# One more unit of filler work ahead of the first attention head in a two-layer transformer kernel

## The chip, the cores and the metric

The kernel runs on one core of one Trainium2 chip. The metric is the device time of one execution in microseconds (us); of several executions the median is given. The core has five engines that run their own instruction queues in order and wait for each other by semaphores: TensorE (PE in the rows; PEld is its weight load), VectorE (DVE), ScalarE (ACT), GpSimd (POOL) and SyncE (SP), which here only issues DMAs.

## The reference

Two layers act on 256 tokens of width 2048, with a context of 256 more. Layer 0 is a Fourier mixer, layer 1 is attention; each has adaptive scale, shift and gate, and an output projection from 4096 to 2048. The change lies in layer 1: 64 query heads of width 64, 8 key/value heads, a sink in the softmax, and the result multiplied by silu(z).

```python
def _attend_with_sink(q, k, v, sink, mask=None):
    s = jnp.einsum('bqhgd,bkhd->bhgqk', q, k).astype(jnp.float32) * (ATTN_HEAD_DIM ** -0.5)
    ...
    p = jax.nn.softmax(jnp.concatenate([s, sk], axis=-1), axis=-1)[..., :-1]
    return jnp.einsum('bhgqk,bkhd->bqhgd', p.astype(v.dtype), v)

def _attention_branch(h, hc, w_in, sink, rows, cols, need_ctx):
    q, k, v, z = jnp.split(h @ w_in, [D_BRANCH, D_BRANCH + kvw, D_BRANCH + 2 * kvw], axis=-1)
    ...
    y = jnp.moveaxis(o, 0, 1).reshape(b, n, D_BRANCH) * jax.nn.silu(z)
```

After it come `y @ w_out[1]`, the gated residual and a final RMS norm. There are 512 keys per query: 256 tokens and 256 of the context.

## The kernel before

Nearly all arithmetic is float32 made of two parts: a weight tile is split into a high part `wh` (a cast on ACT, L66) and a remainder `wl` (a subtraction on DVE, L67), and three matmuls take the place of one (`mm3`, L145 to L147). Some weights of layer 0 and of the key/value projection are split into two float16 parts instead.

The attention stage of layer 1 interleaves two streams of work.

**The filler.** `units()` lists 140 units of projection work. Eight units make the query projection of one key/value head's group of eight query heads ("q"); two units make one 128-wide block of z ("z", L1386 and L1388). The list is q0, q1, z0 to z3, q2, z4 to z7, and so on to q7 and z24 to z31, and then 12 units ("o") of the output projection, each two of the 32 steps `k` of its first 512 columns. `emit_unit()` emits the next unit and prepares the weights of the one after (DMA on SP, cast on ACT, subtraction on DVE). When the list is empty it emits nothing. A unit of q or o is 12 matmuls, a unit of z is 16 shorter ones.

**The heads.** There are 64 heads `i`. `stage_s(i)` computes the scores: four matmuls (L1422, L1423), the mask and the maximum on DVE (L1424), the exponential on ACT (L1427, L1428), the reciprocal of the sum on DVE (L1429, L1430), and the probabilities `f` as two float16 halves, high by ACT (L1439) and low by DVE (L1440), for two blocks of 128 queries each. For the heads below 62, `f` is then transposed into `ft` by two DMA transposes from SP's queue (L1442), one for each query block. For the last two heads the transposes are matmuls on PE (`stage_t`, L1449) and are copied out of PSUM by ACT and DVE (L1450). `stage_o(i)` multiplies `ft` with the values on PE (8 matmuls, L1457 and L1458), and ACT and DVE add the two halves up (L1463, L1464). After every second head, `emit_y` writes a block of y (L1407), which `y_split` later splits into two parts for the output projection; for the steps `k` below 24 POOL makes the remainder (L67 on POOL), above that DVE.

**The order.** First come `first` units with no head beside them; then 66 steps. Step `i` emits `stage_s(i)`, (for the last two heads) `stage_t(i - 2)`, one unit, `stage_o(i - 2)`, and one unit. So 66 steps have 132 places for units, and with 10 ahead there are 142 places for 140 units: the last two places, both in step 65, stay empty. After the steps the code goes on with `k` = 24 to 31 of the same output projection (four more pieces of that work, which need all of y) and then with the other columns.

That is the order in which the code emits. The build then schedules the emitted instructions, engine by engine, by a timeline of its own; the program holds one fixed order per engine. So a place in the emitted list moves what each engine meets, but not one for one.

In the text, "head 0" is `stage_s(0)` and so on; "scores of head i" are its four matmuls, "output of head i" the eight of L1457 and L1458.

Of the kernel before, what the change touches and what calls it, by code (L numbers as in the profile page):

```python
# [32 lines left out]
def tile_dit(ctx: ExitStack, tc: tile.TileContext, a: dict, out: bass.AP):  # L33
# [1102 lines left out]
    with tc.tile_pool(name="h1", reuse_waits="tile", bufs=16) as h1p:  # L1136
# [94 lines left out]
        with tc.tile_pool(name="at", reuse_waits="tile", bufs=2) as at:  # L1231
# [234 lines left out]
                    obs[blk, 1] = ob  # L1466
                    emit_y(blk)

            first = 10
            for i in range(first):  # L1470
                emit_unit()
                if i == 2:
# [249 lines left out]
```

## Time and profile before

| | us |
|---|---|
| median of 3 runs | 1769.35 (1767.74 to 1769.62) |
| the profiled execution, its own time | 1769.55 |
| span of the profile of that execution | 1767.8 |
| attention stage: first scores, last output of a head (start) | 1127.2, 1608.8 |

The span is the time from the first to the last profiled instruction; the execution's own time has 1.75 us more around it. Rows of the timeline view give the start in us from the span's start, the duration in us (of a merged row with "x4" of all four together), the engine, the line, the operation, `out<-in` with the buffer numbers left out, and in square brackets how long the engine was idle just before and what released it. PE's matmuls overlap: the duration of one is longer than the step from one start to the next, so a pace on PE is read from the starts.

### The profile page before, as it was taken

What the parts mean: (1) busy time and instruction counts of PE and PEld (TensorE: products, weight loads), DVE (VectorE), ACT (ScalarE), POOL (GpSimd) and SP (SyncE); (2) the same over time, 40 slices, a digit from 0 to 9 for tenths busy, and PEclk for the clock granted to TensorE, in tenths of its full rate; (3) what the DMA queues carried; (4) which work ended last, traced back from release to release, by engine and by line L of the source; (5) the groups of instructions that cost most, each with busy time, mean ns of one, the idle gap of its engine ahead of it and who ended that gap; (6) DMA issues with size and microseconds to landing.
All of it is one profiled execution on the core that took longest, in us unless ns stands there. A gap on an engine that the chain in (4) does not pass through costs nothing. (4 is left out here: it accounts for less than half of the span.)

```text
span 1767.8 us, 26608 instructions
## 1 busy us (share of the span) xinstructions
PE 1732.2 (98%) x9517; PEld 1187.7 (67%) x9517; DVE 1406.6 (80%) x2454; ACT 1090.5 (62%) x2069; POOL 331.9 (19%) x440
## 2 busy tenths in 40 slices
PE   6999999999999999999999999999999999999997
PEld 4679999644444444446444746788888888887886
DVE  5779889797677786877797695899999989997455
ACT  5545556477777755465223554687888878895343
POOL 0002111212222214212101001302312230233010
PEclk9999999999999999999999999999999999999999
DMA  9998998778998969977996432588988898887543
GB/s 394 417 356 247 279 278 254 289 286 314 332 305 312 312 228 371 368 267 259 341 316 212 142 137 74 169 215 199 223 207 206 213 215 206 207 212 258 190 167 143
DMA packets 229077, 447.29 MB, mean 253 GB/s; under 512 B 155888, under 2 KB 156288, under 8 KB 202064
## 3 DMA queue, kind: packets, MB, share of 16 engines
q1 hardware_dynamic: 182784, 331.93, 58.3%
q0 software_dynamic: 42016, 106.70, 19.4%
q10 hardware_dynamic: 4144, 6.95, 1.2%
q8 instruction: 75, 1.23, 0.3%
q14 instruction: 58, 0.48, 0.1%
HBM read 400.43 MB, written 12.59 MB: 234 GB/s over the span
## 5 line engine op out<-in xcount | busy, mean ns | idle before, releaser
L67 DVE TENSOR_TENSOR wl<-raw,wh 128x1024 fp32r<-128x1024 f32 x197 | 262.5, 1338 | 108.0 <-ACT wh L66 80.3
L66 ACT CAST wh<-raw 128x1024 fp32r<-128x1024 f32 x197 | 205.5, 1044 | 138.1 <-PE ps L146 97.0
L146 PE MATMUL ps<-act,wf 128*128 128x512 f16 x512 | 194.0, 379 | 0.0
L147 PE MATMUL ps<-act,wf 128*128 128x512 f16 x512 | 191.1, 379 | 0.0
L145 PE MATMUL ps<-act,wf 128*128 128x512 f16 x512 | 189.8, 379 | 0.6 <-ACT wf L137 0.2
L1386 PE MATMUL ps<-h,wh 128*128 128x512 f32 x512 | 185.0, 397 | 0.0
L145 PE MATMUL ps<-y,wf 128*128 128x512 f16 x448 | 169.8, 379 | 0.8 <-ACT wf L137 0.8
L147 PEld LDWEIGHTS <-wf 128*128 128x128 f16 x960 | 93.8, 98 | 114.0 <-DVE wf L138 0.9
L146 PE MATMUL ps<-y,wf 128*128 128x512 f16 x448 | 169.8, 379 | 0.0
L145 PEld LDWEIGHTS <-wf 128*128 128x128 f16 x960 | 93.7, 98 | 113.3 <-ACT wf L137 4.2
L147 PE MATMUL ps<-y,wf 128*128 128x512 f16 x448 | 167.4, 379 | 0.4 <-DVE wf L138 0.4
L146 PEld LDWEIGHTS <-wf 128*128 128x128 f16 x960 | 93.9, 98 | 109.0
L137 ACT ACTIVATE wf<-raw,nrm 128x1024 f16<-128x1024 f32 x56 | 63.4, 1145 | 137.1 <-DVE acc L792 68.5
L1388 PE MATMUL ps<-h,wl 128*128 128x256 f32 x512 | 138.6, 281 | 0.0
L138 DVE SCALAR_TENSOR_TENSOR wf<-raw,tn,wf 128x1024 f16<-128x1024 f32 x64 | 79.8, 1281 | 42.0 <-ACT wf L137 41.9
L1440 DVE SCALAR_TENSOR_TENSOR f<-p,sm,f 128x512 f16<-128x512 f32 x128 | 105.8, 847 | 9.0 <-ACT f L1439 8.7
L790 POOL DMA_DIRECT2D wa<-in_adw x64 | 34.0, 532 | 403.2 <-PE ps L147 149.7
L1427 ACT ACTIVATE p<-ps,mx 128x512 f32<-128x512 f32 x128 | 87.9, 689 | 35.0 <-DVE mx L1424 29.6
L1439 ACT ACTIVATE f<-p,sm 128x512 f16<-128x512 f32 x128 | 88.1, 717 | 34.3 <-DMA ft<-f 15.6
L1386 PEld LDWEIGHTS ps<-h,wh 128*128 128x128 f32 x512 | 96.4, 188 | 19.1
L827 ACT ACTIVATE act<-act 128x512 f32<-128x512 f32 x160 | 98.4, 616 | 6.0 <-DMA act<-in_wo 4.5
L146 PE MATMUL ps<-wl,h 128*128 128x512 f32 x256 | 101.3, 396 | 0.0
(414 smaller groups left out, 4672.8 us busy)
## 6 DMA issues: line engine op xcount, KB each, us to landing
raw<-in_wz SPq DMA_DIRECT2D x64, 1024.0 KB, 5.4
raw<-in_awp SPq DMA_DIRECT2D x32, 1024.0 KB, 12.7
zr<-in_adw SPq DMA_DIRECT2D x64, 512.0 KB, 6.8
wa<-in_adw POOLq DMA_DIRECT2D x64, 512.0 KB, 6.5
act<-in_wo POOLq DMA_DIRECT2D x128, 256.0 KB, 7.5
raw<-in_wo SPq DMA_DIRECT2D x32, 1024.0 KB, 7.7
raw<-in_wq SPq DMA_DIRECT2D x32, 1024.0 KB, 5.2
raw<-in_wu SPq DMA_DIRECT2D x32, 1016.0 KB, 6.5
```

Source lines behind the costliest of these rows:

```text
L66: last_cast[0] = S.copy(h, src).ins
L67: last_sub[0] = eng.tensor_tensor(l, src, h.bitcast(F32), op=ALU.subtract).ins
L138: last_sub[0] = V.scalar_tensor_tensor(w[:, 1], src, up, w[:, 0], op0=ALU.mult, op1=ALU.subtract).ins
L145: PE.matmul(o, wh, xh, start=start, stop=False)
L146: PE.matmul(o, wh, xl, start=False, stop=False)
L147: return PE.matmul(o, wl, xh, start=False, stop=stop).ins
L827: S.activation(t, t, AF.Square, accum_out=c)
L1386: PE.matmul(o[0], wh[:, q], hx1[k], start=k == 0, stop=k == KT - 1)
L1388: PE.matmul(o[0][:, 0:N], wl[:, q], hx1[k][:, 0:N], start=False, stop=False)
L1427: S.activation(pt[tb], so[tb], AF.Exp, bias=mx[:, tb : tb + 1], scale=-1.0, accum_out=sm[:, tb : tb + 1])
L1439: S.activation(f[:, 0:512], pt[tb], AF.Copy, scale=sm[:, tb : tb + 1])
L1440: V.scalar_tensor_tensor(f[:, 512:1024], pt[tb], sm[:, tb : tb + 1], f[:, 0:512], op0=ALU.mult, op1=ALU.subtract)
```

## The change

`first` is 11 instead of 10. So one more unit (the third of q1) stands ahead of head 0, every later unit stands one place earlier among the heads, and three places at the end are empty instead of two: the second place of step 64 and both of step 65. No instruction of the computation is added or removed.

```diff
-            first = 10
+            first = 11
             for i in range(first):
                 emit_unit()
                 if i == 2:
```

**Around head 0, on DVE.** The names are: `sm` the softmax sum, `ps`, `mx` the scores being masked and their maximum (L1424, of the third head here, whose row `ISA mx` reads the maximum out), `wl` the remainder of a weight tile, `f` the probabilities of head 0. Before:

```order
L1429 SCALAR_TENSOR_TENSOR sm_10963<-sm_10963,es_10964 128x2
L1424 ISA ps_11087,mx_11084<-ps_11087,mask_9936,nsink_9940 128x512
L1424 ISA mx_11084 128x1
L1430 RECIPROCAL sm_10963<-sm_10963 128x2
L1424 ISA ps_11091,mx_11084<-ps_11091,mask_9936,nsink_9940 128x512
L67 TENSOR_TENSOR wl_11141<-raw_11138,wh_11140 128x1024
L1440 SCALAR_TENSOR_TENSOR f_10979<-p_10960,sm_10963,f_10979 128x512
L1440 SCALAR_TENSOR_TENSOR f_10983<-p_10961,sm_10963,f_10983 128x512
L67 TENSOR_TENSOR wl_11206<-raw_11138,wh_11205 128x1024
```

The same place now:

```order
L1429 SCALAR_TENSOR_TENSOR sm_10979<-sm_10979,es_10980 128x2
L1430 RECIPROCAL sm_10979<-sm_10979 128x2
L67 TENSOR_TENSOR wl_11128<-raw_11125,wh_11127 128x1024
L1440 SCALAR_TENSOR_TENSOR f_10995<-p_10976,sm_10979,f_10995 128x512
L1424 ISA ps_11103,mx_11100<-ps_11103,mask_9936,nsink_9940 128x512
L1424 ISA mx_11100 128x1
L1440 SCALAR_TENSOR_TENSOR f_10999<-p_10977,sm_10979,f_10999 128x512
L1424 ISA ps_11107,mx_11100<-ps_11107,mask_9936,nsink_9940 128x512
L67 TENSOR_TENSOR wl_11179<-raw_11125,wh_11178 128x1024
```

The masking of the third head's scores moved from ahead of both halves of head 0's `f` to between and behind them. On PE the scores of heads 0 and 1 stand where they stood; those of the third head come after 19 matmuls of filler instead of 7; the output of head 0 keeps its place.

**Around the last head, on DVE.** Here `ps_16520` and `ps_16544` are the output of head 61, `sm`, `f` belong to head 63, `ft_16407` and `ft_16429` are the second query block of head 62's transpose, `ft_16491` and `ft_16513` that of head 63's. Before:

```order
L1464 TENSOR_TENSOR ob_16445<-ps_16520,ot_16529 64x256
L1450 COPY ft_16407<-ps_16568 128x8x128
L1429 SCALAR_TENSOR_TENSOR sm_16476<-sm_16476,es_16477 128x2
L1430 RECIPROCAL sm_16476<-sm_16476 128x2
L1407 SCALAR_TENSOR_TENSOR act_16532<-ob_16445,dsc_9946,th_16019 128x256
L67 TENSOR_TENSOR wl_16579<-raw_16534,wh_16578 128x1024
L1440 SCALAR_TENSOR_TENSOR f_16492<-p_16473,sm_16476,f_16492 128x512
L1440 SCALAR_TENSOR_TENSOR f_16495<-p_16474,sm_16476,f_16495 128x512
L67 TENSOR_TENSOR wl_16680<-raw_16677,wh_16679 128x1024
L1464 TENSOR_TENSOR ob_16603<-ps_16594,ot_16604 64x256
L1450 COPY ft_16491<-ps_16629 128x8x128
```

Now:

```order
L1429 SCALAR_TENSOR_TENSOR sm_16498<-sm_16498,es_16499 128x2
L1430 RECIPROCAL sm_16498<-sm_16498 128x2
L1464 TENSOR_TENSOR ob_16469<-ps_16544,ot_16553 64x256
L1407 SCALAR_TENSOR_TENSOR act_16556<-ob_16469,dsc_9946,th_16006 128x256
L67 TENSOR_TENSOR wl_16680<-raw_16677,wh_16679 128x1024
L1440 SCALAR_TENSOR_TENSOR f_16514<-p_16495,sm_16498,f_16514 128x512
L1450 COPY ft_16429<-ps_16584 128x8x128
L1440 SCALAR_TENSOR_TENSOR f_16517<-p_16496,sm_16498,f_16517 128x512
L67 TENSOR_TENSOR wl_16714<-raw_16677,wh_16713 128x1024
L1464 TENSOR_TENSOR ob_16615<-ps_16606,ot_16616 64x256
L1450 COPY ft_16513<-ps_16629 128x8x128
```

The copy of head 62's `ft` moved from ahead of head 63's sum to between the halves of head 63's `f`. On ACT, correspondingly, the second exponential of head 63 moved from behind the copy of `ft` for head 62's first block to ahead of it.

**Around the last head, on POOL.** `act<-act` with L67 is the remainder of a step `k` of y from 16 to 23; L1515, L1510 and L1517 are DMA issues for the end of the kernel. The difference (+ is now):

```order
 L67 TENSOR_TENSOR ys<-act,ys 128x256 x16
-L67 TENSOR_TENSOR act<-act 128x256 x4
+L67 TENSOR_TENSOR act<-act 128x256 x6
 L1515 DMA act<-x1d 128x512 x8
-L67 TENSOR_TENSOR act<-act 128x256 x4
+L67 TENSOR_TENSOR act<-act 128x256 x2
 L1510 DMA gbc<-gated 128x2048
```

Two of the eight subtractions moved from behind the eight DMA issues to ahead of them.

## The prediction

> **What bounds the kernel now.** The page's first part comes first: which engine is busy.
>
> ```profile
> PE 1732.2 (98%) x9517; PEld 1187.7 (67%) x9517; DVE 1406.6 (80%) x2454; ACT 1090.5 (62%) x2069; POOL 331.9 (19%) x440
> ```
>
> PE is the bound of the whole program. The change neither adds nor removes a matmul, so only the time in which PE stands still, or runs at a lower clock, can change. A stretch of the attention stage (columns: the stretch, its length, busy us of PE, PEld, DVE, ACT, POOL, then PE's granted clock, the DMA share and GB/s), and, from the groups of instructions from 1060 us on, the two that split the weights (busy, mean ns | idle before them and its releasers):
>
> ```profile
> 1200.00:1300.00 100.00, 99.29 (x559) 83.12 (x559) 95.01 (x172) 81.63 (x163) 26.70 (x20) 1.00 0.87 210
> ...
> L67 DVE TENSOR_TENSOR wl<-raw,wh 128x1024 fp32r<-128x1024 f32 x189 | 252.7, 1343 | 88.0 <-ACT wh L66 73.4 <-PE ps L147 13.2 <-PE ps L1458 0.7
> L66 ACT CAST wh<-raw 128x1024 fp32r<-128x1024 f32 x189 | 197.1, 1044 | 107.9 <-PE ps L146 83.8 <-PE ps L147 17.8 <-DMA raw<-in_wo1c 3.3
> ```
>
> PE is full, but DVE is at 95%: the softmax of a head and the weight remainders leave DVE little room, and a head whose `ft` comes late stops PE. What DVE does wait for, at its remainders, is mostly ACT's cast, and the cast waits for PE to give a weight buffer back. The view of waits, PE alone, from 1060 to 1620 us (total, times, longest):
>
> ```profile
> PE ps L1457 <- DMA ft<-f: 4.2, 4, 2.0
> PE ps L1457 <- DVE ft L1450: 1.7, 1, 1.7
> PE ps L1449 <- DVE f L1440: 0.9, 1, 0.9
> ```
>
> Six waits, 6.8 us in all, every one in the heads' transposes or what follows them. That is nearly the whole stake of this change. The timeline of PE says where they are; the first, with the stretch around it:
>
> ```profile
> 1139.36 0.27 PE L1457 MATMUL ps<-ft,v 128*128 128x256 f16 x1 [2.03 <-DMA ft<-f]
> 1139.47 0.27 PE L1458 MATMUL ps<-ft,v 128*128 128x256 f16 x1
> 1142.50 0.63 PE L1386 MATMUL ps<-h,wh 128*128 128x512 f32 x1
> 1142.92 0.35 PE L1388 MATMUL ps<-h,wl 128*128 128x256 f32 x1
> 1143.11 0.40 PE L1386 MATMUL ps<-h,wh 128*128 128x512 f32 x1
> ...
> 1139.00:1143.00 4.00, 3.64 (x14) 2.84 (x15) 4.00 (x7) 2.22 (x6) 4.00 (x3) 0.58 0.87 286
> ```
>
> PE waits 2.03 us for head 0's `ft`, and then the clock is 0.58 over 4 us: a 512-wide matmul steps by 0.42 us (1142.50 to 1142.92). At the full pace, 0.23 us for a 512-wide f32 matmul, 0.12 for a 256-wide one and 0.11 for the outputs (1139.36 to 1139.47), the work from 1139.36 to 1143.11 (8 outputs, 4 scores, one z pair) is 0.88 + 0.92 + 0.35 = 2.15 us; it took 3.75. So this place costs 2.0 + 1.6 = 3.6 us.
>
> **The change part by part.**
>
> *Head 0.* Its output stands where it stood on PE, so the question is when its second DMA transpose lands. The chain now:
>
> ```profile
> 1129.26 0.40 PE L145 MATMUL ps<-wh,h 128*128 128x512 f32 x1
> 1129.49 0.40 PE L146 MATMUL ps<-wl,h 128*128 128x512 f32 x1
> ...
> 1130.74 1.04 ACT L66 CAST wh<-raw 128x1024 fp32r<-128x1024 f32 x1
> 1131.32 0.76 DVE L1424 CUSTOM_DVE_ANT_0 ps<-ps,mask,nsink 128x512 f32<-128x512 f32 x1
> 1132.53 1.33 ACT L1439 ACTIVATE f<-p,sm 128x512 f16<-128x512 f32 x2
> 1132.73 1.22 DVE L67 TENSOR_TENSOR wl<-raw,wh 128x1024 fp32r<-128x1024 f32 x1
> 1133.86 1.41 DVE L1440 SCALAR_TENSOR_TENSOR f<-p,sm,f 128x512 f16<-128x512 f32 x2
> 1134.68 2.71 SPq L1442 DMA_TRANSPOSE ft<-f  x2
> ```
>
> Now the remainder `wl` can follow its cast at 1131.8 and end by 1133.0 (1.2 us). The low half of `f` needs ACT's high half, whose place on ACT did not change: 1132.53 + 0.67 = 1133.2. So DVE's first half runs 1133.2 to 1133.9 (0.7 us) and the first transpose is issued 0.7 us earlier, near 1134.0. Then the third head's first masking steps in. Its scores come 12 matmuls later, 12 x 0.23 (1129.26 to 1129.49) = 2.8 us, so it can start at 1131.32 + 2.8 = 1134.1; the second half of `f` follows at 1134.8 and ends at 1135.5, against 1135.3 now. SP's queue spends 1.35 us on each issue (2.71 for two): the second is issued now near 1136.05, then near 1135.6. It lands 0.45 us earlier, and the wait falls to about 1.6 us. Bounds: nothing gained, if landing does not follow issue; 0.7, if the masking does not hold the second half up.
>
> Whether the slow stretch goes with it decides more than that. The nearest rows stand at the end of the stage:
>
> ```profile
> 1606.09 0.40 PE L1449 MATMUL ps<-ident,f 128*128 128x128 f16 x4 [0.91 <-DVE f L1440]
> 1608.15 0.28 PE L1457 MATMUL ps<-ft,v 128*128 128x256 f16 x1 [1.67 <-DVE ft L1450]
> ...
> 1605.00:1610.00 5.00, 2.42 (x21) 1.83 (x19) 3.46 (x5) 1.69 (x3) 1.52 (x3) 1.00 1.00 354
> ```
>
> Waits of 0.91 and 1.67 us within 3 us left the clock at 1.00. A wait of 1.6 is nearer to these than to 2.03, so I take the slow stretch as gone: 1.6 us, bounds 0 and 1.6. Head 0 together: -0.4 - 1.6 = -2.0. The Trainium skill (TensorE: Matmul & The Clock Gate, Part 1) says that PE falls to half its clock after an idle window of about 3.4 us, and that the window runs free of the program. The stretch at 0.58 is about as long as such a window, but the wait before it is shorter, so here the trace goes further than the rule. By the rule alone a 2.03 us wait costs no clock and head 0 gives 0.4; by a free window it could also differ between executions.
>
> *Heads 1 to 60.* Two more waits (heads 14 and 39; the first row is the second transpose of head 14), and an ordinary head, 24, in a phase in which the filler is a query projection (scores, its two transposes, output):
>
> ```profile
> 1238.54 3.28 SPq L1442 DMA_TRANSPOSE ft<-f  x1
> 1244.50 0.27 PE L1457 MATMUL ps<-ft,v 128*128 128x256 f16 x1 [0.71 <-DMA ft<-f]
> 1432.57 0.27 PE L1457 MATMUL ps<-ft,v 128*128 128x256 f16 x1 [0.61 <-DMA ft<-f]
> ...
> 1301.43 0.39 PE L1423 MATMUL ps<-kkl,qa 128*128 128x512 f32 x1
> 1311.01 3.20 SPq L1442 DMA_TRANSPOSE ft<-f  x2
> 1319.25 0.28 PE L1457 MATMUL ps<-ft,v 128*128 128x256 f16 x1
> ```
>
> The waiting transpose landed 5.96 us after its issue, 3.28 of it the issue, so about 2.7 behind it. In the ordinary head issue ends at 1314.2, landing is near 1316.9, and 2.3 us are to spare. The new order is not a plain shift here. In phases with z, scores and outputs alternate with 16 matmuls between them as before. In each query phase, 25, 22 and 16 matmuls in turn stand between a head's scores and the next output, where 11 or 12 stood: counted at the paces above, the three heads scored around the phase's start get 18.5 to 21.1 us of PE work between scores and output instead of 17.5 to 18.0, and the fourth gets 17.1 instead of 17.5. The two waiting heads are among the first three, so 0.71 + 0.61 = 1.3 us should go, and the fourth loses 0.5 of its 2.3 us. Against it: PE reaches heads 2 to 14 about 2 us earlier, and DVE at 95% may not follow. I take 1.3 won and 1.0 given back, -0.3; bounds -1.3 and, as below, +7.9.
>
> *The last heads.* PE's first wait here is for head 61; the rest is the chain of head 63:
>
> ```profile
> 1593.82 0.40 PE L1423 MATMUL ps<-kkl,qb 128*128 128x512 f32 x1
> 1595.05 0.27 PE L1457 MATMUL ps<-ft,v 128*128 128x256 f16 x1 [0.83 <-DMA ft<-f]
> 1597.16 1.01 ACT L1450 COPY ft<-ps 128x1024 f16<-128x1024 f16 x1
> 1598.07 0.70 ACT L1427 ACTIVATE p<-ps,mx 128x512 f32<-128x512 f32 x1
> 1599.40 0.69 DVE L1450 COPY ft<-ps 128x1024 f16<-128x1024 f16 x1 [1.17 <-PE ps L1449]
> 1600.01 0.15 DVE L1429 SCALAR_TENSOR_TENSOR sm<-sm,es 128x2 f32<-128x2 f32 x1
> 1601.80 0.74 DVE L1440 SCALAR_TENSOR_TENSOR f<-p,sm,f 128x512 f16<-128x512 f32 x1
> 1602.46 3.57 DVE L1440 SCALAR_TENSOR_TENSOR f<-p,sm,f 128x512 f16<-128x512 f32 x1
> 1602.69 2.78 POOL L67 TENSOR_TENSOR act<-act 128x256 fp32r<-128x256 f32 x4
> 1607.43 0.67 DVE L1450 COPY ft<-ps 128x1024 f16<-128x1024 f16 x1
> ```
>
> From the end of head 63's scores (1594.05) to its output (1608.15) go 14.1 us. Two things on that chain move. The second exponential no longer stands behind ACT's 1.01 us copy, and the sum no longer behind DVE's copy, which waited 1.17 us for PE: about 2 us earlier. And the second half of `f` took 3.57 us where its twin took 0.74, in the time in which POOL did four subtractions; of these only two are left behind the DMA issues, 1.4 us. Laid out anew from the end of the scores: sum at 3.4, `wl` 4.8 to 6.0 behind its cast, first half of `f` 6.4 to 7.1, copy of head 62's `ft` 8.0 to 8.7 behind PE's transposes, second half 8.7 to 9.4, or 10.1 with POOL in the way; PE then reaches head 63's transposes (10.2 us of its own work and the wait for head 61), ends them near 11.2, DVE's copy ends at 12, the output starts near 12.3. That is 1.8 us less. Bounds: -3.4 (all waits here) and +1 (behind the output PE has 8 matmuls of filler left instead of 20, 8 x 0.23 = 1.9 us, before it needs the first of `k` = 24 to 31, whose split also stands behind the output). The Trainium skill (SBUF — State Buffer, 🔬 SBUF: two separate sides) says that DVE and GpSimd share a port pair as an exclusive lock, and the loser blocks for the whole instruction. The 3.57 us row agrees, and by it a POOL subtraction moved forward may block a DVE step of head 62 instead: nothing of this would be won.
>
> **Sum.** Against the profiled execution, 1769.55: -2.0 - 0.3 - 1.8 = -4.1, that is 1765.45; it lies 0.2 above the median shown, so 1765.3 by the median (-0.23%). What a measurement of this kernel can tell from no change is about 0.2%, 3.5 us: the forecast lies just beyond.
>
> **The rivals.**
>
> *What head 0 wins is lost again (about 1768).* For it: DVE at 95%, and head 14 waits already in the old order. Then PE's 2.0 us return as waits at heads 2 to 14 and only the end gives, 1.8 us less: 1767.6. The same time comes out if the slow stretch stays and the end wins half: -0.4 - 0.3 - 0.9, 1767.8. Against it: DVE's own waits hang on casts that wait for PE, so DVE moves forward with PE.
>
> *Each query phase brings waits (slower, 1773.4).* Six phases of a query projection have the uneven order. If in each of them two heads wait as long as the two rows of 0.71 and 0.61, that is 6 x 1.32 = 7.9 us on top of -2.0 - 1.8: +4.1. It decides from 0.6 us a phase on. For it: bunched DVE work with 5% to spare, and a transpose that takes 3.3 us to issue at head 14 and 1.35 at head 0. Against it: the first query phase has an order of this kind already in the old program, and PE waits nowhere there.
>
> *The order hardly matters (1769).* Head 0 still waits 2 us, the end still blocks on POOL.
>
> **How the numbers follow.** Forecast 0.52; won and lost again 0.24; waits in each query phase 0.18; no effect 0.06. The forecast's own range is 1763 to 1767; part of it lies within 0.2%, and part of the first rival beyond. Low end of the range: all waits of head 0 and the end gone, 1762; high end: most of the third case, 1772.5. Faster by over 0.2%: 0.52; within: 0.29; slower: 0.19.
>
> **What would show it.** Right: the wait before the first L1457 is below 1.7 us and the granted clock behind it 1.00; no wait near heads 14 and 39; from head 63's last L1423 to its first L1457 about 12.3 us; the second half of its `f` below 2.2 us. Wrong: a wait over 2 us at head 0, waits in each query phase, or PE idle between the last output and `k` = 24.

## The result, and the profile after

The changed kernel is slower: 1785.98 us (median of 4 runs, 1783.01 to 1786.93) against 1768.55 us for the kernel before (4 runs, 1765.78 to 1769.62). The ratio is 1.0099, with a 95% interval of 1.0084 to 1.0115. Forecast were 1765.3 us and a range of 1762 to 1772.5. Three executions with a mean granted clock of 0.56 to 0.66 (one of experiment 4, two of the kernel before beside experiments 1 and 2) took 2515 to 2954 us and are in no median or ratio below.

The page of the changed kernel; its profiled execution took 1786.93 us:

```profile
span 1785.0 us, 26554 instructions
PE 1735.8 (97%) x9517; PEld 1189.6 (67%) x9517; DVE 1420.9 (80%) x2454; ACT 1088.5 (61%) x2069; POOL 337.7 (19%) x440
```

As many matmuls as before on a span that is 17.2 us longer: PE stood still, or ran slower. The view of stretches says how much of it in the attention stage. This is its sum over 1060 to 1630 us (570 us), first of the kernel before:

```profile
sum 570.00, PE 563.16 PEld 456.80 DVE 504.99 ACT 437.68 POOL 140.60; mean PE 93.86 PEld 76.13 DVE 84.17 ACT 72.95 POOL 23.43
```

and of the changed kernel:

```profile
sum 570.00, PE 550.40 PEld 445.28 DVE 506.10 ACT 426.03 POOL 143.17; mean PE 91.73 PEld 74.21 DVE 84.35 ACT 71.01 POOL 23.86
```

PE is busy 12.8 us less in the same 570 us; DVE is as busy as before. What PE waits for (waits view, PE, 1060 to 1640 us; total, times, longest):

```profile
PE ps L1457 <- DMA ft<-f: 18.6, 10, 4.7
PE ps L1457 <- DVE ft L1450: 1.0, 1, 1.0
```

Waits for `ft` from the DMA transposes were 4.2 us in 4 places; now they are 18.6 us in 10. PE's timeline says where: heads 0, 13, 29, 45, 53, 61 and 63 (not shown: 1.89 us at head 37 and 0.5 to 0.9 at heads 23, 32 and 39):

```profile
1139.03 0.27 PE L1457 MATMUL ps<-ft,v 128*128 128x256 f16 x1 [1.42 <-DMA ft<-f]
...
1242.89 0.27 PE L1457 MATMUL ps<-ft,v 128*128 128x256 f16 x1 [2.36 <-DMA ft<-f]
...
1367.55 0.27 PE L1457 MATMUL ps<-ft,v 128*128 128x256 f16 x1 [1.80 <-DMA ft<-f]
...
1493.86 0.27 PE L1457 MATMUL ps<-ft,v 128*128 128x256 f16 x1 [2.25 <-DMA ft<-f]
...
1555.66 0.40 PE L1457 MATMUL ps<-ft,v 128*128 128x256 f16 x1 [4.72 <-DMA ft<-f]
...
1616.61 0.28 PE L1457 MATMUL ps<-ft,v 128*128 128x256 f16 x1 [1.95 <-DMA ft<-f]
...
1628.13 0.28 PE L1457 MATMUL ps<-ft,v 128*128 128x256 f16 x1 [1.00 <-DVE ft L1450]
```

Stretches just behind the waits of heads 0, 13, 45 and 53 (PE's granted clock is the third number from the end):

```profile
1139.00:1143.00 4.00, 3.97 (x26) 3.54 (x27) 4.00 (x5) 2.53 (x6) 4.00 (x3) 1.00 0.78 277
1243.00:1247.00 4.00, 4.00 (x16) 3.26 (x15) 3.96 (x6) 3.58 (x6) 0.68 (x1) 0.58 0.95 294
1494.00:1498.00 4.00, 4.00 (x23) 3.30 (x22) 3.75 (x5) 2.90 (x6) 1.02 (x1) 1.00 1.02 288
1556.00:1561.00 5.00, 5.00 (x20) 4.05 (x18) 4.23 (x9) 3.75 (x9) 0.00 (x0) 0.50 0.97 254
```

Head 63's output starts 20.0 us later than before (1628.13 against 1608.15). Of this 2.8 us are the unit moved ahead (12 matmuls at 0.23) and come back behind it. The waits are 12.8 us more (19.6 against 6.8). Clock below full costs 3.4 us more, counted in steps of 2 us (length times one minus clock): 5.1 at heads 13 and 53 against 1.7 at head 0 before. The first scores start 0.3 us later (1127.48 against 1127.20). That is 19.3; where the remaining 0.7 goes is not shown. So the loss sits along the heads, above all at 13, 29, 37, 45 and 53, each the head number 5 of its group of eight (counted from 0). Head 21, in the same place, does not wait: its second transpose is issued by 18.5 us after its scores, and PE has 20.8 us of work up to its output.

**One such head read through.** Head 29 on DVE, before. Its scores end at 1339.05 (start of the last L1423 plus 0.23); columns as in the timeline, L1424 is the masking, L1440 the low half of `f`:

```profile
1340.03 0.74 DVE L1424 CUSTOM_DVE_ANT_0 ps<-ps,mask,nsink 128x512 f32<-128x512 f32 x1
...
1342.16 0.74 DVE L1424 CUSTOM_DVE_ANT_0 ps<-ps,mask,nsink 128x512 f32<-128x512 f32 x1
...
1343.00 0.69 DVE L1310 TENSOR_TENSOR qa<-ps,qa 64x512 fp32r<-64x512 f32 x1
...
1346.80 0.17 DVE L1430 RECIPROCAL sm<-sm 128x2 f32<-128x2 f32 x1
...
1350.56 0.75 DVE L1440 SCALAR_TENSOR_TENSOR f<-p,sm,f 128x512 f16<-128x512 f32 x1
```

The same head in the changed kernel, where its scores end at 1344.75:

```profile
1344.80 1.23 DVE L67 TENSOR_TENSOR wl<-raw,wh 128x1024 fp32r<-128x1024 f32 x1 [0.28 <-ACT wh L66]
1345.94 0.42 DVE L1393 TENSOR_TENSOR zs<-ps,zs 128x256 f32<-128x256 f32 x1
1346.39 0.68 DVE L1310 TENSOR_TENSOR qa<-ps,qa 64x512 fp32r<-64x512 f32 x1
1347.09 0.69 DVE L1311 TENSOR_TENSOR qb<-ps,qb 64x512 fp32r<-64x512 f32 x1
1347.81 1.41 DVE L1440 SCALAR_TENSOR_TENSOR f<-p,sm,f 128x512 f16<-128x512 f32 x2
...
1349.93 0.74 DVE L1424 CUSTOM_DVE_ANT_0 ps<-ps,mask,nsink 128x512 f32<-128x512 f32 x1
...
1351.74 0.75 DVE L1424 CUSTOM_DVE_ANT_0 ps<-ps,mask,nsink 128x512 f32<-128x512 f32 x1
...
1356.22 0.17 DVE L1430 RECIPROCAL sm<-sm 128x2 f32<-128x2 f32 x1
...
1358.36 1.23 DVE L67 TENSOR_TENSOR wl<-raw,wh 128x1024 fp32r<-128x1024 f32 x1
1359.50 1.41 DVE L1440 SCALAR_TENSOR_TENSOR f<-p,sm,f 128x512 f16<-128x512 f32 x2
```

Before, the first masking starts 1.0 us after the scores end; now 5.2 us. The scores come later against the filler's work on DVE: ahead of the first masking stand a remainder, a z block's sum, two subtractions of the query turn (`qa`, `qb`: the turn is what makes a finished query projection ready for the scores; PE transposes it at L1305, ACT casts it at L1308 and L1309, and DVE makes the remainders at L1310 and L1311) and both halves of head 28's `f`. Before, those subtractions stood behind the maskings. Between the scores and the last low half stand four remainders instead of two (not all shown). The last low half starts 11.5 us after the scores before and, half of the merged row on, 15.4 us now.

Then SP's queue. Before (the weight load, L50, and the first transpose):

```profile
1346.01 0.33 SPq L50 DMA_DIRECT2D raw<-in_wq  x1
1349.64 1.23 SPq L1442 DMA_TRANSPOSE ft<-f  x1
```

Now:

```profile
1359.62 0.33 SPq L50 DMA_DIRECT2D raw<-in_wq  x1
1360.33 5.13 SPq L1442 DMA_TRANSPOSE ft<-f  x2
```

The remainder at 1358.36 was the last reader of a weight buffer. As soon as it ends, SP issues the next load of 1 MB, 0.7 us ahead of the transposes, and the second transpose then takes 3.80 us to issue (it starts at 1361.65) where it took 1.23. So the sum from scores to output is 16.9 + 3.8 + 2.1 = 22.8 us now against 12.3 + 1.2 + 4.5 = 18.0 before (scores to second issue, issue, end of issue to output). The last term is spare time, and 2.1 us is what remains when PE waits. Two things are late there, one behind the other: DVE's order, and a load that DVE's order lets go at the wrong moment. Head 53 has the same order on DVE and is as late (16.9 + 3.4 = 20.3 us to the end of the second issue), but behind the last query projection its filler is z alone: 17.7 us of PE work, so it waits 4.72 us. The experiments take the two apart.

### The profile page after: what moved, and what is told of

Its sections match the earlier page's. It is cut to its first block, busy times and chain, and to the rows that moved or that the text cites. A ratio compares the mean times of both kernels' runs of the same rounds, so it can differ in the third digit from the quotient of the medians.

```text
span 1785.0 us, 26554 instructions
## 1 busy us (share of the span) xinstructions
PE 1735.8 (97%) x9517; PEld 1189.6 (67%) x9517; DVE 1420.9 (80%) x2454; ACT 1088.5 (61%) x2069; POOL 337.7 (19%) x440
## 3 DMA queue, kind: packets, MB, share of 16 engines
q8 instruction: 75, 1.23, 0.3%
## 5 line engine op out<-in xcount | busy, mean ns | idle before, releaser
L67 DVE TENSOR_TENSOR wl<-raw,wh 128x1024 fp32r<-128x1024 f32 x197 | 260.8, 1326 | 106.5 <-ACT wh L66 80.5
L1440 DVE SCALAR_TENSOR_TENSOR f<-p,sm,f 128x512 f16<-128x512 f32 x128 | 110.2, 883 | 13.9 <-ACT f L1439 13.4
L1386 PEld LDWEIGHTS ps<-h,wh 128*128 128x128 f32 x512 | 97.1, 190 | 19.3
L147 PE MATMUL ps<-wh,h 128*128 128x512 f32 x256 | 101.4, 397 | 0.0
```

Of the source, the lines that this page charges most:

```text
L67: last_sub[0] = eng.tensor_tensor(l, src, h.bitcast(F32), op=ALU.subtract).ins
L147: return PE.matmul(o, wl, xh, start=False, stop=stop).ins
L1386: PE.matmul(o[0], wh[:, q], hx1[k], start=k == 0, stop=k == KT - 1)
L1440: V.scalar_tensor_tensor(f[:, 512:1024], pt[tb], sm[:, tb : tb + 1], f[:, 0:512], op0=ALU.mult, op1=ALU.subtract)
```

## The experiments

All edits are made to the kernel before; where `first = 11` stands in them, they contain the change. All ratios are to runs of the kernel before on the same chip. In the expectations, "fifth to seventh head" means the heads with number 5 to 7 in a group that counts from 0, and the letters are theories: A, PE loses at the heads all along the stage; B, at the start; C, at the end; D, the loss grows with every unit ahead; E, it is the place of the query turn. The other letters are explained where they stand.

**1. Which part of the stage.** The extra unit ahead, and one place left empty again in step 0, in step 32, or (with ten ahead) one unit more at step 58:

```diff
-            first = 10
+            first = 11
...
-                filler()
+                if i != 0:
+                    filler()
```

> Eleven units ahead, but the second place of step 0 stays empty, so every unit from step 1 on stands where it stood in the kernel before; head 0 and the third head's scores are moved as in the change. Theory A (the loss of 17 us is made at heads 1 to 61, because each unit falls on the other half of its step, all along the stage): within 3 us of before, 1765 to 1770, and no wait of PE for a transpose over 1 us between heads 10 and 60. Theory B (the one unit more ahead of head 0 is what costs, through what it sets off at the start): 1780 or more. If my reckoning of head 0 held, its wait falls from 2.0 to about 1.5 us.

> Eleven units ahead, and the second place of step 32 left empty: the units of steps 0 to 32 stand as in the change, those behind as before. Theory A: the waits of the change at heads 13, 23, 29 and 32 stay (some 6 us and one stretch at a lower clock), those at heads 37, 45 and 53 go; 1774 to 1778. Theory B: as the change, 1784 to 1787. Theory C (the end is what costs): as before, 1766 to 1770.

> Ten units ahead, and one unit more in step 58: only the last steps are as in the change. Theory A: within 3 us of before, by my reckoning of the last heads up to 1.8 us faster, 1765 to 1769. Theory C (the emptied place at the end costs, or the uneven last phase): 1774 or more.

Measured: 1766.95 us (12 runs), ratio 0.999 (0.998 to 1.0), for the shift that is undone at once; 1775.51 (6 runs), 1.0042 (1.0029 to 1.0056), for the shift that holds through half of the steps; 1770.96 (12 runs), 1.0014 (0.9999 to 1.0029), for the shift of the end alone. The loss goes with the number of steps that run shifted, so A holds and B and C fall. And the end gives nothing: my gain of 1.8 us there is not seen. The first of these kernels says nothing on head 0's part. Against what I expected, it has the order of the kernel before there: the third head's scores start 3.45 us after head 0's (before 3.46, changed 6.26), and their masking stands ahead of head 0's `f` again. Head 0's output in it, and the stretch behind it:

```profile
1140.93 0.27 PE L1457 MATMUL ps<-ft,v 128*128 128x256 f16 x1 [2.02 <-DMA ft<-f]
```

```profile
1141.00:1145.00 4.00, 4.00 (x25) 3.50 (x25) 4.00 (x7) 2.22 (x6) 4.00 (x4) 1.00 0.90 292
```

The wait is as long as in the kernel before (2.03) and not 1.5 us, yet the clock stays at 1.00; the last section says why.

**2. Other shifts.** `first = 12` and `first = 9`, nothing else:

> Twelve units ahead: every unit one whole step earlier, so on the same half of a step as in the kernel before. Theory A in its plain form (the half of the step decides): within 5 us of before, 1764 to 1774. Theory D (each unit ahead of its place costs, whichever half of the step it falls on): about twice the change's loss, 1795 to 1805.

> Nine units ahead: every unit one place later than in the kernel before, the other half of the step again, and head 0 has less filler ahead. Theory D (units ahead of their place cost, the later the better): 1768 or less, but for head 0, whose softmax has the same 9 us of PE work. Theory A with the place of the units against the heads (any other place than that of before lets some heads' ft come late): 1773 to 1790, with PE waits for ft that return every eight heads.

Measured: 1793.65 us, 1.0148 (1.0131 to 1.0166), and 1792.83 us, 1.0139 (1.0114 to 1.0163), 4 runs each. Both neighbours are slower, with waits for `ft` of 23.2 and 23.8 us. So it is no growing loss (D falls), and the half of the step on which a unit falls does not decide either: twelve, on the same half as ten, was expected at 1764 to 1774. Of the four places tried, ten is the one at which the steps of the heads and of the filler fit.

**3. The place of the query turn.** With eleven ahead, the turn one place later, or sooner:

```diff
-                if defer and defer[0][0] + 2 < j:
+                if defer and defer[0][0] + 3 < j:
```

> As the change, but the transposes of the next group's queries (q_turn) are put off by one unit more, so that DVE's four subtractions for qa and qb (0.7 us each) stand, against the heads, where they stood before the change. Theory E (these subtractions, now ahead of the masks and the sums of the heads scored at a query phase's start, are what makes ft late there): most of the loss goes, 1768 to 1773, no PE wait over 1 us at heads 13, 29, 37, 45 and 53. Rival F (the whole of DVE's queue, with z and the weight remainders, is rearranged; the subtractions are a small part): 1780 to 1788.

> Eleven units ahead, and the transposes, casts and subtractions of a finished query projection are let go one place sooner. Theory T (place of the turn in the step: before, both turns stand in the same step, in the changed kernel in two): both in one step again, so 1766 to 1772. Theory Q-order: DVE work between first masking and last f is 9.9 and 10.5 us at the fifth and sixth head but 6.8 at the seventh, against 10.9, 10.5, 9.8 in the changed kernel, so the time lies between, 1772 to 1782.

Measured: later, 1792.87 us, 1.014 (1.0114 to 1.0167), with waits for `ft` of 21.8 us; sooner, 1777.39 us, 1.0054 (1.0038 to 1.0071), with 6.5 us and a new wait of 3.6 us for POOL's rope. The place of the turn matters, but putting it back into the place that it has before (later) does not bring the time back, so E as the only cause falls. At the heads number 5 it did what E says: the waits at 13, 29, 37, 45 and 53 fall to 0.7 us and less. But others open one to three heads on (1.3 us at heads 16 and 24, 3.0 at 32, 1.6 at 40, 1.2 at 48). Sooner, both turns in one step, gives half of the loss back: not the 1766 to 1772 of theory T, but inside the 1772 to 1782 that the order on DVE let expect.

**4. One step more between scores and output.** Output three steps behind its scores, `ft` with four buffers, and for space `qa` and `qb` with two:

```diff
-                ft = at.tile([P, 8, 2, P], F16, tag="ft", name="ft", bufs=3)
+                ft = at.tile([P, 8, 2, P], F16, tag="ft", name="ft", bufs=4)
...
-                    stage_o(i - 2, *pts.pop(i - 2))
+                    stage_o(i - 3, *pts.pop(i - 3))
```

> As the change (eleven units ahead), but the output of a head stands three steps behind its scores instead of two: 7 us more for the softmax and the transposes, with a fourth ft buffer, and two qa and qb buffers instead of three to make room. If ft that comes late is the whole loss (theory A): the waits at heads 13 to 53 go, 1764 to 1772. If DVE as a whole cannot keep up with the new order (rival G): PE waits as long, at the same heads or for weight remainders, 1780 or more.

> The same three steps with ten units ahead, as the control: theory A expects e6 and this within 4 us of each other, this one between 1762 and 1769 because the waits of the kernel before at heads 0, 14 and 39 (3.4 us, and 1.6 of lower clock) go; rival G expects this one near 1768 and e6 at 1780 or more.

Measured: 1787.38 us, 1.0112 (1.0089 to 1.0135), and 1786.22 us (3 runs), 1.0109 (1.0083 to 1.0135). The control is as slow as the other, so this edit costs some 19 us by itself, and the time says nothing on the question. Why it costs that stays open; buffers for `qa` and `qb` went down with it. But the waits of the kernel with eleven, 1060 to 1640 us, show what is late once `ft` has more time:

```profile
PE ps L1388 <- DVE wl L67: 10.0, 8, 2.0
PE ps L146 <- DVE wl L67: 3.3, 4, 1.1
```

No head's output waits for a DMA transpose any more, and PE waits 13.3 us for remainders instead.

**5. Room on DVE.** Only 128 of 1024 columns of a z unit's remainder are computed, and all eight of its matmuls with the remainder use these; the other columns are left out. With ten and with eleven ahead:

```diff
-            split(h, l, t[:, i * 1024 : (i + 1) * 1024])
+            last_cast[0] = S.copy(h, t[:, i * 1024 : (i + 1) * 1024]).ins
+            last_sub[0] = V.tensor_tensor(l[:, 0:n], t[:, i * 1024 : i * 1024 + n], h[:, 0:n].bitcast(F32), op=ALU.subtract).ins
...
-                                PE.matmul(o[0][:, 0:N], wl[:, q], hx1[k][:, 0:N], start=False, stop=False)
+                                PE.matmul(o[0][:, 0:N], wl[:, 0:P], hx1[k][:, 0:N], start=False, stop=False)
```

> Of the 64 z units' remainders only the first 128 of 1024 columns are computed, and all eight matmuls of a z unit use these; buffers and matmuls are as many as before. DVE saves about 64 x 1.0 us in the attention stage. It is the control for the same with eleven units ahead. Theory Q (in the changed kernel the order puts more DVE work ahead of some heads' softmax, and DVE at 95% has no room for it): nearly all waits for ft are gone here too, about 1760 to 1764. Theory S (what is late is the transposes on SP's queue, behind the weight loads): the waits stay as they are, about 1768.

> The same with eleven units ahead. Theory Q: with room on DVE the place of the units no longer matters: within 0.3% of the control with ten, under 3 us of waits for ft in heads 1 to 62, and the second transpose issued less than 14 us after the scores at every kind of head. Theory S: still some 15 us (0.9%) slower than the control, with waits for ft at heads 13, 29, 45, 53 as in the changed kernel.

Measured: 1763.23 us, 0.9973 (0.9958 to 0.9987), with ten, and 1765.43 us, 0.9987 (0.9975 to 1.0), with eleven: the price of the change falls from 17.4 us to 2.2. The waits of the kernel with eleven (line numbers are 4 higher), 1060 to 1640 us:

```profile
PE ps L1461 <- DMA ft<-f: 3.5, 3, 1.5
PE ps L1461 <- DVE ft L1454: 1.3, 1, 1.3
```

DVE is busy 457.7 us in the 570 instead of 506.1, the second transpose issues 8.7 us after the scores at the heads number 5 (15.8 in the changed kernel), and its issue takes 1.45 us there instead of 3.53. So DVE without room is a condition for the loss.

**6. The loads away from SP's queue.** The weight loads of the stage issued from POOL's queue (the line for the o units, changed alike, is not shown):

```diff
-                    raws1[src] = raw(a["wq"][n, i // 2] if kind == "q" else a["wz1"][n])
+                    raws1[src] = raw(a["wq"][n, i // 2] if kind == "q" else a["wz1"][n], nc.gpsimd)
```

> The weight loads of the attention stage (q, z and o units) are issued from POOL's queue, so that SP's queue holds the transposes alone. Control for the same with eleven units. Theory S: the second transpose issues in 1.3 us at every head, the four waits for ft of before go, about 1764. Theory Q: no change on DVE, 1766 to 1772; loads may come later where POOL is busy with the rope.

> The same with eleven units ahead. Theory S: within 0.3% of its control with ten, the waits for ft at heads 13 to 53 gone, as the 2 to 3 us by which the second transpose's issue is longer there make the whole wait. Theory Q: still 12 to 18 us slower than its control, the second transposes still issued over 15 us after the scores at the fifth to seventh head of each group of eight, whatever their own issue takes.

Measured: 1792.35 us, 1.0143 (1.0106 to 1.0179), and 1813.92 us, 1.0259 (1.0231 to 1.0288). Eleven still costs 21.6 us over ten. The second transposes do not issue faster: 2.78 us on average in the control, where the kernel before has 2.20. So sharing a queue with the loads is not what makes the issue long, and S falls in this form. The control itself is 25 us slower than the kernel before, with 18.4 us of waits for `ft`, where both theories had it at 1772 us or less; why was not looked into, so the pair speaks on the issue alone. The Trainium skill (DMA: Bandwidth & Descriptors, 🎯 Rules for kernel authors) says that spreading DMAs over issuing engines brings no bandwidth, since all use the same 16 DMA engines; no run here measures the bandwidth, but an issue that is as long behind a load of another queue fits it.

**7. DVE's order, by force.** One edge in each step: the remainder that the second place prepares stands behind the low half of the head before (two kernels, eleven and ten ahead); or, the other way, the remainder of the first place behind the masking of the same step:

```diff
-                    ready[pos[0] + 1] = prep(ulist[pos[0] + 1])
+                    with tc.issue_after(behind[0]) if behind[0] else nullcontext():
+                        ready[pos[0] + 1] = prep(ulist[pos[0] + 1])
...
+                behind[0] = low.get(i - 1) if i < 60 else None
                 filler()
```

> The changed kernel (eleven units ahead) with one edge more in each step on DVE: the remainder that the step's second place prepares is queued behind the low half of f of the head before. Nothing is left out. Theory Q-order (DVE's order makes ft late): from head 24 on the DVE work between a head's first masking and its last f is 5.5 to 9.8 us in the program's order where the changed kernel has 5.8 to 10.9, and so the waits for ft from there on should be at most half of the changed kernel's, and the time 1766 to 1775. Theory Q-total (only how much DVE has to do counts): the waits stay, 1783 to 1788.

> Control: the same edge with ten units ahead. From head 9 on the order on DVE is as without it, so 1765 to 1770 by either theory; only the first heads could move.

> Eleven units ahead, and the remainder of the step's first place is queued behind the masking of the same step's head. In the program's order the DVE work between first masking and last f grows to 14.4, 13.1, 8.6, 11.0, 11.9 us at the fifth to ninth head of a group. Theory Q-order: slower still than the changed kernel, 1790 to 1805. Theory Q-total: no change, 1783 to 1788.

Measured: 1781.79 us, 1.0081 (1.0064 to 1.0098); 1772.12 us, 1.0024 (1.0015 to 1.0034); 1811.62 us, 1.0249 (1.023 to 1.0268). The waits of the first (line numbers 2 higher):

```profile
PE ps L1459 <- DMA ft<-f: 5.8, 5, 2.8
PE ps L1390 <- DVE wl L67: 3.7, 6, 1.2
PE ps L146 <- DVE wl L67: 1.6, 2, 0.8
```

The waits for `ft` fall from 18.6 to 5.8 us, as the order theory says, and DVE's total is the same (504.9 us in the 570). But what is put behind is late next: PE now waits 5.3 us for remainders, so the time falls by only 4 us, hardly clear of the intervals (1.0064 to 1.0098 against 1.0084 to 1.0115), and the 1766 to 1775 that I expected was missed. The control with ten pays 3.06 us for a remainder at head 0, with a slow stretch behind it, and was expected some 2 us faster. The order for the worse costs 26 us more than the change itself, beyond the 1790 to 1805 expected, with DVE as busy over the whole program (1420.8 us, 1420.9 in the changed kernel): the same work in another order does that. At the heads number 5 something else shows: the second transpose issues as late as in the changed kernel (15.3 us after the scores, 15.8 there) and yet four of these six heads wait 0.2 us or not at all (13 and 53 wait 1.0 and 1.3), since its issue takes 1.42 us instead of 3.53. The load now comes behind the transposes.

**8. The load behind the transposes.** Each load of a q or z unit stands on SP's queue behind the second transpose of the head three steps back:

```diff
-                    raws1[src] = raw(a["wq"][n, i // 2] if kind == "q" else a["wz1"][n])
+                    with tc.issue_after(turned[0]) if turned[0] else nullcontext():
+                        raws1[src] = raw(a["wq"][n, i // 2] if kind == "q" else a["wz1"][n])
...
+                turned[0] = second.get(i - 3)
```

> Eleven units ahead, and on SP's queue each weight load of a q or z unit stands behind the second transpose of the head three steps back, so that no load is issued just ahead of a pair of transposes. At the fifth head of a group the DVE work between first masking and last f stays at 10.9 us in the program's order; behind it the order gets shorter (9.4 and 6.8 us at the sixth and seventh, against 10.5 and 9.8). Theory L (the waits at the fifth heads are the long issue of the second transpose behind a load): the second transpose issues in 1.3 to 1.5 us there, the waits at heads 13, 21, 29, 37, 45, 53 fall below 0.5 us, and the time is 1766 to 1774. Theory Q-order without L: waits of 1 us and more stay at these heads, 1776 to 1784.

> The same with ten units ahead; DVE's order is that of before from head 13 on. Theory L: the second transposes issue in 1.3 to 1.5 us everywhere (2.20 on average before), the two waits at heads 14 and 39 go, 1764 to 1768. Theory Q-order without L: as before, 1766 to 1770. If holding the loads back makes weights late, PE waits for wl or the cast waits for raw and both are slower.

Measured: 1785.0 us, 1.0101 (1.0086 to 1.0116), with eleven; 1765.23 us, 0.9982 (0.997 to 0.9995), with ten. With eleven the issue at the heads number 5 is 1.54 us (3.53 before this edit), and the waits at heads 13, 29, 37, 45 and 53 fall from 2.36, 1.80, 1.89, 2.25 and 4.72 us to 1.51, 0.91, 0.90, 0.58 and 2.38; new ones open at heads 21 (0.92) and 38 (1.10). Neither theory is right alone: with the shorter issue the five waits fall by 0.9 to 2.3 us, and the rest stays, since `f` itself is late. Of the 5.8 us less that PE waits at heads 1 to 60, 2.4 come back at head 61 (4.31 us, with a stretch at half clock behind it) and 1.9 as waits for POOL's rope and a remainder; the time stays. With ten, the waits for the DMA transposes of heads 14, 39 and 61 are gone (line numbers 2 higher):

```profile
PE ps L1459 <- ACT act L1292: 2.0, 1, 2.0
PE ps L1459 <- DVE ft L1452: 1.1, 1, 1.1
PE ps L146 <- DVE wl L67: 0.2, 1, 0.2
```

The first row is head 0. Its wait is there as before (2.01 us, before 2.03): the view names a copy on ACT that ended just ahead, but the output also starts 1.95 us after the end of its second transpose's issue (1137.28 to 1139.23), as in the kernel before (1137.39 to 1139.36, 1.97). The second transposes issue in 1.45 us on average instead of 2.20. This kernel leaves nothing out and is faster than the kernel before by 3 us (0.18%, interval 0.05% to 0.3%).

The numbers side by side; the middle columns are means over the heads number 5 and 6 of the groups, heads below 62, from the timeline's rows:

| kernel | us | PE busy in 570 us | scores to second issue, number 5, 6 | its issue, number 5, 6 |
|---|---|---|---|---|
| before | 1768.55 | 563.2 | 13.3, 12.1 | 1.53, 1.93 |
| changed | 1785.98 | 550.4 | 15.8, 16.0 | 3.53, 2.51 |
| changed, room on DVE | 1765.43 | 565.2 | 8.7, 8.1 | 1.45, 1.38 |
| changed, remainder behind `f` | 1781.79 | 556.6 | 15.3, 13.9 | 1.42, 2.29 |
| changed, turn sooner | 1777.39 | 556.3 | 14.2, 14.1 | 3.40, 1.33 |
| changed, load behind transposes | 1785.0 | 552.0 | 16.2, 14.1 | 1.54, 2.45 |
| ten, load behind transposes | 1765.23 | 566.7 | 12.5, 11.7 | 1.25, 1.25 |

What is shown: the shift costs time all along the stage, needs a full DVE, and works through DVE's order and, for a part, through the load. What stays open: no edit that keeps eleven units ahead and leaves nothing out brought back more than half of the loss, so how the loss divides between the order and the load is known only for single heads.

## Why the prediction was wrong

**What bounds the kernel: right.** PE full, DVE at 95%, and a late `ft` stops PE. Room on DVE took nearly all of the loss away.

**Head 0: right, by the numbers.** The wait was forecast at about 1.6 us and is 1.42, and the clock behind it is 1.00. Less the 0.3 us of the later start, the chain came as laid out: masking at 1134.1, second half of `f` at 1134.8, second issue at 1135.6. The reason for the clock was weaker than it looked: a wait of 2.02 us in the first experiment left the clock alone too. A wait of 1.42 us lies below all that cost clock in these runs (last section), so the result was sound; that the old wait of 2.03 us did cost clock was in part luck. What the place is worth alone no run shows.

**Heads 1 to 60: the step that failed.** It was forecast at -0.3 us; measured are 13.9 us more of waits for `ft` from head 1 to head 60 (15.2 now, 1.3 before) and 5.1 us of slow clock that was not there. The step counted PE's work between a head's scores and its output, found more of it at the three heads around a query phase (18.5 to 21.1 us instead of 17.5 to 18.0), and took this as slack. The PE side came true: head 29 has 21.0 us of work there (22.8 less the wait of 1.80), against 18.0. What was left out is the other side of the same race. DVE meets the same shift: PE does the scores of these heads later against the filler, so that the masking stands behind a query turn's subtractions and the `f` of the head before, and more of the remainders stand ahead of its own `f`. At head 29 the slack grew by 3 us, and the chain to the end of the second issue by 7.2 (20.7 against 13.5 us); at head 53 the slack did not grow at all (17.7 against 18.0). The opening was too narrow as well: the six old waits, 6.8 us, were called nearly the whole stake, but they bound only what can be won, not what can be lost. The order on DVE was there to be read at these heads, as it was read at head 0 and at the last one. The prediction also took the 3.28 us issue at head 14 and the 1.35 us at head 0 as a spread without a cause; it has one, below.

**The rival on this side was named, and too small.** "Each query phase brings waits" had the mechanism, bunched work on a full DVE, and 7.9 us as its price, from the two waits of 0.71 and 0.61 us in the old trace. Now the six phases have 0, 2.4, 0.9, 2.7, 2.4 and 2.3 us: 10.5 in all, not far from the price. What the rival lacked is head 53, which stands in no such phase (4.7 us), and the slow clock behind heads 13 and 53 (5.1 us). The argument against it was that the first query phase had such an order and no wait. Head 5 of the kernel before shows why: its second issue ended 20.2 us after its scores (16.64 + 3.56), nearly as late as head 29's now, but 23.6 us of PE work stood up to its output, and not 21.0. The wait was spared by PE's work there, not by DVE.

**The last heads: the sum did not move.** Forecast from the end of head 63's scores to its output were 12.3 us; it is 13.6 (1628.13 less 1614.50), against 14.1. Head 63's chain in the changed kernel, on DVE:

```profile
1619.33 0.36 DVE L1429 SCALAR_TENSOR_TENSOR sm<-sm,es 128x2 f32<-128x2 f32 x1
...
1623.23 0.75 DVE L1440 SCALAR_TENSOR_TENSOR f<-p,sm,f 128x512 f16<-128x512 f32 x1 [0.43 <-ACT f L1439]
...
1624.50 0.97 DVE L1440 SCALAR_TENSOR_TENSOR f<-p,sm,f 128x512 f16<-128x512 f32 x1
1625.40 1.75 DVE L67 TENSOR_TENSOR wl<-raw,wh 128x1024 fp32r<-128x1024 f32 x1
...
1627.40 0.67 DVE L1450 COPY ft<-ps 128x1024 f16<-128x1024 f16 x1
```

and POOL's subtractions beside it:

```profile
1615.97 3.70 POOL L67 TENSOR_TENSOR act<-act 128x256 fp32r<-128x256 f32 x4 [19.23 <-ACT act L66]
...
1624.19 1.87 POOL L67 TENSOR_TENSOR act<-act 128x256 fp32r<-128x256 f32 x2 [0.21 <-ACT act L66]
```

The long second half of `f` is gone as forecast (0.97 instead of 3.57 us). But the sum comes 4.8 us after the scores and not 3.4, since head 63's two maskings stand behind a remainder, with a half of head 62's `f` behind each, and the first half at 8.7 and not 6.4, behind ACT's copy of head 62's `ft`. Head 62's two halves took 1.03 and 1.24 us (at 1616.21 and 1617.83) where 0.74 is usual, while POOL did four subtractions. That is 0.8 us, a part of what was not won. It fits the rule that spoke against this step, the exclusive lock of the Trainium skill (SBUF — State Buffer, 🔬 SBUF: two separate sides). How much of this the order decides is open: the first experiment's kernel has the order of the kernel before at the end on DVE and POOL, and there head 63's two halves took 1.88 us together instead of 4.24 and the whole stretch 11.7 us, as POOL's four subtractions started later against them (1601.84, the halves at 1600.27; before 1602.69 and 1601.80).

**The sum.** Head 0 gave 2.3 us (0.6 of its wait and 1.7 of clock; 2.0 were forecast), the last heads 0.5 of 1.8 from scores to output (head 61's wait, 1.1 us longer, is in it), and heads 1 to 60 cost 19.0 instead of winning 0.3: 16.2 us slower. With the 0.3 us of the later start and the 0.7 not traced that is the 17.2 by which the two spans differ. So the step on heads 1 to 60 is nearly the whole error.

## What to carry to other kernels

When two streams are interleaved and the second engine is at 95%, a shift of one against the other is a new order on every engine, all along the stage. Read the order of the full engine at the repeating place (here one group of eight heads), from scores to transposes, and add its durations up; slack counted on PE alone is half of the race. A big load that is let go when a buffer falls free can land just ahead of a small transfer on the critical path: holding it back behind that transfer gave 3 us here with ten units ahead, and with eleven nothing, since DVE was late itself.

## What the runs showed of the hardware that was not expected

**The issue of a DMA transpose behind a load.** The second transpose of a pair (128x1024, two bytes each) mostly takes 1.23 to 1.4 us to issue (2.1 at most) when the last weight load (128x2048 of four bytes) was issued over 4 us ahead, and about 3 us when it was 1 to 3 us ahead. By the distance from the end of the load's issue to the start of the transpose's: 1 to 2 us, 3.56 us on average over 7 heads before and 3.19 over 9 in the changed kernel; 2 to 3 us, 2.59 over 25 and 2.94 over 18; 4 to 6 us, 1.29 over 12 and 1.39 over 23 (between 3 and 4 us both kinds occur). With the loads on POOL's queue the issue is no shorter (2.78 us on average) and goes by the same distance: 4.23 us over 18 at 1 to 2 us, 1.29 over 11 at 4 to 6. No run says what the issue waits for in the engines that move the data.

**The clock after a wait.** Waits of 2.03 (before), 2.36 (head 13) and 4.72 us (head 53) were followed by 0.58, 0.58 and 0.50 of the clock over 4 to 5 us; waits of 2.02 (first experiment) and 2.25 us (head 45) by 1.00. So about 2 us of standing still does it at one time and not at another. The stretches at heads 0 (before) and 13 cost 1.7 us each, which is 3.4 us at half clock, and the one at head 53 twice that. In the changed kernel's profile the half-clock stretches start at 1243.67, 1554.28 and, behind the stage, 1779.56 us, which is 91 and 66 steps of 3.413 us apart; in every other profile with more than one they lie on such a grid too. On this grid, heads 13 and 45 of the changed kernel look like this (behind the comma PE's busy time, third from the end its clock):

```profile
1240.25:1243.66 3.41, 1.05 (x10) 0.78 (x9) 1.85 (x3) 2.62 (x6) 3.01 (x2) 1.00 1.05 200
1243.67:1247.08 3.41, 3.41 (x11) 2.74 (x9) 3.38 (x6) 2.91 (x6) 0.01 (x1) 0.50 1.03 308
...
1489.43:1492.84 3.41, 2.18 (x10) 1.52 (x9) 2.78 (x6) 3.25 (x7) 1.26 (x1) 1.00 1.22 224
1492.84:1496.25 3.41, 2.39 (x15) 2.04 (x15) 2.78 (x4) 2.97 (x6) 2.12 (x2) 1.00 0.88 257
```

Head 13's wait lies whole in one window, and the next one runs at half clock; head 45's wait, nearly as long, is cut in two. In the attention stage of 19 profiles (all but that of the control in experiment 4) there are 26 windows at full clock in which PE stood still for 2.1 us or more, and each is followed by one at half clock; of the 111 with 0.8 to 1.9 us one is, and of the 4 with 1.99 to 2.03 us three. Of the 41 half-clock windows, the 30 in which PE stood still for 0.6 us or less were followed by the full clock, the 11 with 0.8 us or more by another at half clock. So what costs clock is about 2 us of standing still inside one window, and where the grid lies differs from execution to execution. The Trainium skill (TensorE: Matmul & The Clock Gate, Part 1) has the half clock after at least one idle window of about 3.4 us and says that the window runs free of the program. Its length and the free grid agree with these traces; that about 2 us of standing still in it are enough, only the traces show.
